# Hybrid block on one core: three weight blocks split early, the mixer's stages in another order

## The chip, the cores and the metric

The kernel runs as one program, launched once, on one core of a Trainium2 chip. The metric is device time in microseconds (us) for the whole program. TensorE (PE) multiplies matrices, VectorE (DVE) and ScalarE (ACT) work on elements, GpSimd (POOL) as well and more slowly, and SyncE (SP) issues most of the DMA transfers. Each engine runs its own instructions strictly in the order in which the program was built; a semaphore wait holds everything behind it on that engine.

## The reference

One residual block on x of 512 frames by 1024 channels, in float32. A gated feed-forward, a mixer and a second gated feed-forward each stand between two RMS norms:

```python
f = swiglu(rmsnorm(x, ffn1_norm_pre[l]), ffn1_w_gu[l], ffn1_w_down[l])
x = x + 0.5 * rmsnorm(f, ffn1_norm_post[l])
m = hybrid_mixer(rmsnorm(x, mix_norm_pre[l]), w_in[l], ...)
x = x + rmsnorm(m, mix_norm_post[l])
f = swiglu(rmsnorm(x, ffn2_norm_pre[l]), ffn2_w_gu[l], ffn2_w_down[l])
x = x + 0.5 * rmsnorm(f, ffn2_norm_post[l])
```

The mixer projects h with `w_in` and splits the columns. Half A is a recurrence with 8 heads of 64 channels, half B a gated, causal, depthwise convolution of width 31 with a layer norm. Both halves go through the output projection `w_out`. The recurrence, for each head and frame:

```python
sz = jnp.einsum('bhij,bhj->bhi', state, z_t)
state = (state * w_t[:, :, None, :]
         + sz[..., None] * b_t[:, :, None, :]
         + v_t[..., None] * k_t[:, :, None, :])
y_t = jnp.einsum('bhij,bhj->bhi', state, r_t)
```

## The kernel before

**Stages.** By time in the profiled execution: the first feed-forward's up products (0 to 241 us), its down product (to about 355, with the norms to 384), the mixer (to about 655), the first column half of the output projection (to 669.6) and the second (to 694), the second feed-forward's up products (to 925) and down product (to 1052).

**Weights.** All large weights lie in DRAM as blocks of 128x1024 float32 (512 KB). `wload` loads one block, `wblock` splits it: ScalarE casts it to a high part (`whi`), VectorE subtracts that from the raw block and gets the low part (`wlo`); with `eng` GpSimd does it instead. `mm3` makes a float32 product of three matmuls, on lines L129, L132 and L133: high by high, low by high, high by low. One block against 512 frames is 24 matmuls of 128x512. `preload` does the same for blocks that a stage needs at its start (`lraw`, `lhi`, `llo`).

**Mixer.** The 8 heads go in four pairs (0 to 3) and two groups of two pairs, G0 and G1; the convolution's 512 channels in four tiles, c0 to c3. A projection block of `w_in` feeds one of key, receptance, value of a pair, or one half of a conv tile's gate. Names in `PLAN`, in the order in which the stages are written:

- `li`, `lg`: the low-rank inputs and the output gate; `p0` to `p3`: projection, token shift (L501 on ScalarE, L502 on VectorE) and score products of a pair. On TensorE the scores are L799 and L807 (out of `bk` and `z`), then L817 (64x64, 128 of them in the trace for a pair) and the value products L778, L779; L783 is the bonus sum, L723 and L725 the decay and rate.
- `c0` to `c3`: a conv tile; `p` puts its 30 shifted multiplications on ScalarE (`cpr`, L681) and the additions on GpSimd (`cacc`, L682), `t` puts the greater part on VectorE (L674).
- `s0`, `s1`: the triangular solve of a group on VectorE (L853 to L870). It reads N, which is sent through DRAM (md, nd, N, D).
- `e0`, `e1`: the solved blocks go through DRAM again (rd, td, Mt, T); TensorE then makes e.P (L903, 32x32 products out of Mt) and, after a copy by ScalarE, e.R (L910, 32x32).
- `k0`, `k1`: combine, L932 (called k.W) and L941 (k.A) on TensorE, masks and sums E on VectorE (L945). `b0`, `b1`: the chain over the 8 chunks (L961, L966) and the heads' norms. `O`, `g0`, `g1`, `x`, `w0`: the conv's norm, mixing, and the start of the output projection.

**What sets the order.** A list scheduler at build time gives each engine one fixed order out of dependencies and a priority per instruction. Priority follows `PLAN`: an item written later comes later, `/n` moves an item by n, `@m` sets it to that of mark m (`m0`, `m1`), and tables such as `O_ST` or `O_CC` move parts of an item. Thus an item that stands later in `PLAN` fills in wherever an earlier one waits.

**Output projection.** The four blocks of the first half are used as 2, 3, 0, 1 (`W_ORDER`); GpSimd makes the low part of blocks 0 and 3 (`POOL_WO`). The second half's four blocks are preloaded raw and split, in the same order. The kernel's norm after it reads the first half's PSUM banks (L252, L256) while the second half begins; PSUM tiles of one tag share two or three buffers (`psum`). Loads on SyncE's queue keep their written order (`load`), also those of x and of the second feed-forward.

Of the kernel before, what the change touches and what calls it, by code (L numbers as in the profile page):

```python
# [8 lines left out]
F32 = mybir.dt.float32  # L9
F32R = mybir.dt.float32r  # L10
# [3 lines left out]
ALU = mybir.AluOpType  # L14
# [4 lines left out]
P = 128  # L19
# [66 lines left out]


def wload(c, i, tag=None):
    if tag is None:
        raw = c.wp.tile([P, 1024], F32, name="wraw", tag="raw", bufs=c.nraw)  # L90
    else:
        raw = slot(c, [P, 1024], F32, "lraw", tag)
    load(c, raw, c.A["w"][i])
    return raw


def wblock(c, i, hi=None, lo=None, raw=None, prev=None, aprev=None, eng=None):

    nc = c.nc
    if raw is None:  # L100
        raw = wload(c, i)
# [349 lines left out]

def ffn_down(c, wbase, gs, gpost, scale, finish, xin, ahead=None):

# [54 lines left out]
DQ = False  # L508
PLAN = 'li p0 p1 c0t320/1000 m1 m0 s0/800 p2 c2p/0 c1p/300 p3 e0@1 s1@0 k0 lg b0 c3t256/600 e1/-150 k1/150 x O g0 b1 w0 g1'
T_SOLVE = ('CB', 'AA')  # L510
T_COMB = ('B', 'A')
COMB_LAG = 3
POOL_PROJ = ()
POOL_WO = (0, 3)
ACT_M = (3, 0, 0, 0)
O_PK = (0, 0, 0, 100)
O_PR = (200, 0, 0, 0)
O_PW = (0, 0, 0, 0)
O_HO = (0, 0, 0, 400)
O_CP = (0, -150)  # L520
O_ST = (-60, 0, -300, 200)
O_CC = (200, -60)
O_SC = (0, 0, 40, -300)
O_PV = (-150, 0, 40, -150)
O_N = (40, 0)
O_T = (-300, 200)
T_PR = 'BBBBC'
# [573 lines left out]
def body(es, tc, A, O, first=True, mixer=True, second=True):  # L1101
# [25 lines left out]
    with phase():  # L1127
# [44 lines left out]

        ffn_down(c, 0, gs, gpo, 0.5, fin, lambda t: load(c, x[t], A["x"][t * P : t * P + P, :]), ahead)
        led = [psum(c, [P, SEQ], tag) for tag in LEAD]
# [145 lines left out]
```

## Time and profile before

| what | value |
|---|---|
| runs (3): median, lowest, highest | 1056.44, 1051.72, 1057.47 us |
| profiled execution, its time | 1054.72 us |
| its span, first to last instruction | 1052.9 us |
| mean granted TensorE clock | 0.981 of full |
| TensorE / VectorE / ScalarE / GpSimd busy | 96% / 74% / 46% / 14% |
| DMA traffic | 107.77 MB, mean 102 GB/s |

Times in the rows are from the span's start. In a timeline a row is one instruction or a run of like ones; the bracket at its end tells how long the engine had been idle before it and what ended that. "PEclk" in windows is the granted clock, 1.00 for full speed; the brackets `(x75)` are counts of instructions.

### The profile page before, as it was taken

How to read it: one execution, taken by the hardware profiler on the slowest of the kernel's cores; microseconds unless marked ns; L12 is line 12 of the kernel's file. 1: busy time of each engine (PE TensorE's matmuls, PEld its weight loads, DVE VectorE, ACT ScalarE, POOL GpSimd, SP SyncE). 2: the span in 40 equal slices, each digit the busy share in tenths (PEclk: the TensorE clock that was granted, in tenths of full speed). 3: DMA queues.
4: the chain of work that ended last, by engine and by line, in shares of the span. 5: the costliest groups of instructions: out<-in, count | busy, mean ns of one | idle time of the engine just before them, and what ended most of it. 6: DMA issues, size and time to landing. Idle time of an engine off the chain costs nothing.

```text
span 1052.9 us, 18597 instructions
## 1 busy us (share of the span) xinstructions
PE 1011.4 (96%) x7570; PEld 892.1 (85%) x7570; DVE 777.1 (74%) x1392; ACT 484.8 (46%) x724; POOL 147.0 (14%) x164
## 2 busy tenths in 40 slices
PE   8999999999999899989988898999999999999997
PEld 8899999998888787757667676788999999988885
DVE  5799989985334756789568797687999899853335
ACT  7453444443224435665766375433534444432232
POOL 0000000000000020365788380000000000000000
PEclk9999999999999999999996989999999999999999
DMA  5233333324425221212420310722333333234231
GB/s 200 81 121 104 117 101 107 100 96 145 150 89 185 86 81 62 77 56 80 91 72 22 61 62 5 271 86 82 120 103 118 101 107 100 96 131 144 89 118 80
DMA packets 54589, 107.77 MB, mean 102 GB/s; under 512 B 28776, under 2 KB 28904, under 8 KB 54504
## 3 DMA queue, kind: packets, MB, share of 16 engines
q1 hardware_dynamic: 53640, 103.96, 30.9%
q10 hardware_dynamic: 864, 2.63, 0.7%
q8 instruction: 59, 0.97, 0.4%
q14 instruction: 26, 0.21, 0.1%
HBM read 98.69 MB, written 7.88 MB: 101 GB/s over the span
## 4 chain that ended last, share of the span: by engine, by line
PE 81%; DVE 10%; ACT 3%; DMA 3%; issue 1%; POOL 1%; SPq 0%; DVEq 0%; ACTq 0%; POOLq 0%
PE ps L129 25%; PE ps L133 25%; PE ps L132 25%; DVE ps L674 1%; DVE wlo L108 1%; PE ps L941 1%; PE ps L817 1%; DMA lraw<-w 1%; POOL cacc L682 1%; DMA D<-nd 1%; DVE E L945 1%; ACT cacc L1033 1%; PE ps L194 1%; DVE llo L108 0%; ACT whi L105 0%
## 5 line engine op out<-in xcount | busy, mean ns | idle before, releaser
L108 DVE TENSOR_TENSOR wlo<-wraw,whi 128x1024 fp32r<-128x1024 f32 x103 | 129.2, 1254 | 138.2 <-ACT whi L105 137.8
L129 PE MATMUL ps<-hT,whi 128*128 128x256 f32 (+1 forms) x600 | 196.2, 329 | 1.1 <-ACT hT L179 0.7
L105 ACT CAST whi<-wraw 128x1024 fp32r<-128x1024 f32 x105 | 110.2, 1050 | 184.9 <-PE ps L132 107.5
L133 PE MATMUL ps<-hT,whi 128*128 128x256 f32 (+1 forms) x600 | 194.4, 326 | 0.4 <-DVE hT L186 0.2
L132 PE MATMUL ps<-hT,wlo 128*128 128x256 f32 (+1 forms) x600 | 194.2, 325 | 0.3 <-DVE ms_s L164 0.3
L682 POOL TENSOR_TENSOR cacc<-cacc,cpr 128x512 f32<-128x512 f32 (+2 forms) x120 | 128.6, 1071 | 33.3 <-ACT cpr L681 25.0
L129 PEld LDWEIGHTS ps<-hT,whi 128*128 128x128 f32 x600 | 114.9, 192 | 14.8 <-issue 3.1
L133 PEld LDWEIGHTS ps<-hT,whi 128*128 128x128 f32 x600 | 114.4, 191 | 11.8 <-issue 1.7
L132 PEld LDWEIGHTS ps<-hT,wlo 128*128 128x128 f32 x600 | 115.0, 192 | 10.4 <-issue 1.5
L132 PE MATMUL ps<-whi,gh 128*128 128x512 f32 x288 | 112.0, 389 | 0.0
L133 PE MATMUL ps<-wlo,gh 128*128 128x512 f32 x288 | 112.0, 389 | 0.0
L681 ACT ACTIVATE cpr<-gpad,vecs 128x512 f32<-128x512 f32 (+2 forms) x120 | 71.1, 601 | 37.4 <-POOL cacc L682 37.0
L132 PE MATMUL ps<-tsum,slo 128*128 128x256 f32 x288 | 80.0, 283 | 0.0
L133 PE MATMUL ps<-tsum,shi 128*128 128x256 f32 x288 | 80.0, 283 | 0.0
L129 PE MATMUL ps<-tsum,shi 128*128 128x256 f32 x288 | 76.3, 283 | 0.0
L129 PE MATMUL ps<-whi,gh 128*128 128x512 f32 x288 | 71.5, 389 | 0.0
L133 PEld LDWEIGHTS ps<-wlo,gh 128*128 128x128 f32 x288 | 54.1, 188 | 11.2
L132 PEld LDWEIGHTS ps<-whi,gh 128*128 128x128 f32 x288 | 54.1, 188 | 11.2
L129 PEld LDWEIGHTS ps<-whi,gh 128*128 128x128 f32 x288 | 53.9, 188 | 11.1
L132 PEld LDWEIGHTS ps<-tsum,slo 128*128 128x128 f32 x288 | 55.3, 192 | 0.0
L133 PEld LDWEIGHTS ps<-tsum,shi 128*128 128x128 f32 x288 | 55.3, 192 | 0.0
L365 ACT CAST shi<-s 128x1024 fp32r<-128x1024 f32 x36 | 37.8, 1050 | 36.0 <-DVE s L358 22.1
(273 smaller groups left out, 2328.0 us busy)
## 6 DMA issues: line engine op xcount, KB each, us to landing
wraw<-w SPq DMA_DIRECT2D x105, 512.0 KB, 3.6
lraw<-w SPq DMA_DIRECT2D x57, 512.0 KB, 3.7
x<-x SPq DMA_DIRECT2D x8, 512.0 KB, 4.5
xs<-x SPq DMA_DIRECT2D x8, 512.0 KB, 2.6
x<-xs SPq DMA_DIRECT2D x8, 512.0 KB, 6.3
gain<-gains ACTq DMA_DIRECT2D x5, 512.0 KB, 5.2
out<-x SPq DMA_DIRECT2D x3, 512.0 KB, 2.6
N<-md SPq DMA_DIRECT2D x4, 256.0 KB, 3.6
```

The lines of the kernel that those rows point to most:

```text
L105: c.last_hi = nc.scalar.copy(hi, raw)
L108: c.last_lo = (eng or nc.vector).tensor_tensor(lo, raw, hi, ALU.subtract)
L129: i = nc.tensor.matmul(out, lhsT=lh, rhs=rh, start=start, stop=False)
L132: nc.tensor.matmul(out, lhsT=ll, rhs=rh, start=False, stop=False)
L133: return nc.tensor.matmul(out, lhsT=lh, rhs=rl, start=False, stop=stop)
L194: i = c.nc.tensor.transpose(out=pt[:, k], in_=self.xn[t][:, kk * P : (kk + 1) * P], identity=c.ident)
L365: nc.scalar.copy(sh, sums)
L674: self.dve_queue(nc.vector.scalar_tensor_tensor(dst, gp[:, j : j + n], dw[:, j : j + 1], lo, ALU.mult, ALU.add), False)
L681: nc.scalar.mul(pr, gp[:, n + j : j + SEQ], dw[:, j : j + 1])
L682: self.pool_queue(nc.gpsimd.tensor_tensor(hi, hi, pr, ALU.add), j == 1)
L817: nc.tensor.matmul(ps[s][dst[par], cc, r], lhsT=bk[g, c0 + cc, s], rhs=E[g, l, par, c0 + cc, 1] if r else I2[g], start=True, stop=True)
L941: nc.tensor.matmul(pa[par][:, cc].rearrange("p a b -> p (a b)"), lhsT=Z_[g, d0 + cc].rearrange("p a b -> p (a b)"), rhs=L_[g, d0 + cc].rea ...
```

## The change

Three blocks of the second half of the output projection (column half two, blocks 0, 1 and 2) are loaded, split and stored to DRAM in the first feed-forward's down product, on GpSimd's DMA queue; block 3 is still loaded raw. The second half then loads high and low parts. `PLAN` puts `p3` ahead of `c1`, `lg` ahead of `k0`, and other offsets follow. `ACT_M` takes four copies of pair 0's masks from ScalarE (the multiplications on VectorE then cover whole tiles), `POOL_PROJ` gives one low part in the projection to GpSimd, `POOL_WO` takes one of two in the output projection away from it.

```diff
+PRE = (26, 27, 28)
+PRE_AT = (1, 3, 5, 7, 9, 11, 13, 15, 17)
+
+def preread(c, todo):
+    if todo:
+        raw = slot(c, [P, 1024], F32, "praw", "sr")
+        c.nc.gpsimd.dma_start(raw, c.A["w"][todo[0]])
+        c.ready.append((todo.pop(0), raw))
+
+def presplit(c, todo):
+    nc = c.nc
+    i, raw = c.ready.pop(0)
+    hi, lo = slot(c, [P, 1024], F32R, "phi", "tmp"), slot(c, [P, 1024], F32R, "plo", "tmp")
+    after(c, nc.scalar.copy(hi, raw), c.last_hi)
+    after(c, nc.vector.tensor_tensor(lo, raw, hi, ALU.subtract), c.last_lo)
+    d = [c.dp.tile([P, 1024], F32, name=f"sp{i}_{n}") for n in range(2)]
+    nc.gpsimd.dma_start(d[0], hi.bitcast(F32))
+    nc.gpsimd.dma_start(d[1], lo.bitcast(F32))
+    c.split[i] = d
+    preread(c, todo)
+
 def wload(c, i, tag=None):
+    if i in c.split:
+        return None
...
 def wblock(c, i, hi=None, lo=None, raw=None, prev=None, aprev=None, eng=None):
+    if i in c.split:
+        if hi is None:
+            c.turns = c.turns % 3 + 1
+            hi, lo = (c.wp.tile([P, 1024], F32R, name="w" + n, tag="raw" if c.turns == 3 else n, bufs=2) for n in ("hi", "lo"))
+        load(c, hi.bitcast(F32), c.split[i][0])
+        load(c, lo.bitcast(F32), c.split[i][1])
+        return hi, lo
...
+    if todo:
+        preread(c, todo), preread(c, todo)
     for k in range(NF - NS):
         w = wblock(c, wd + k)
+        if c.ready and k in PRE_AT:
+            presplit(c, todo)
...
-PLAN = 'li p0 p1 c0t320/1000 m1 m0 s0/800 p2 c2p/0 c1p/300 p3 e0@1 s1@0 k0 lg b0 c3t256/600 e1/-150 k1/150 x O g0 b1 w0 g1'
+PLAN = 'li p0 p1 c0t320/0 s0/800 m1 m0 p2 c2p/600 p3 c1p/600 e0@1 lg k0@1 s1@0 b0 c3t256/0 e1/-400 x k1@1 g0/400 O b1 w0/800 g1'
...
-COMB_LAG = 3
-POOL_PROJ = ()
-POOL_WO = (0, 3)
-ACT_M = (3, 0, 0, 0)
+COMB_LAG = 4
+POOL_PROJ = (11,)
+POOL_WO = (0,)
+ACT_M = (1, 0, 0, 0)
...
-O_ST = (-60, 0, -300, 200)
-O_CC = (200, -60)
+O_ST = (-150, -300, 40, 200)
+O_CC = (400, 0)
...
-        ffn_down(c, 0, gs, gpo, 0.5, fin, lambda t: load(c, x[t], A["x"][t * P : t * P + P, :]), ahead)
+        ffn_down(c, 0, gs, gpo, 0.5, fin, lambda t: load(c, x[t], A["x"][t * P : t * P + P, :]), ahead, [NB_FFN + n for n in PRE])
```

The other tables (`O_PR`, `O_HO`, `O_CP`, `O_PV`, `O_N`, `O_T`) change in the same way.

**TensorE, pair 2's last score products, 489 to 492 us in the trace.** L817 are these products, L129, L132 and L133 the wide ones of a projection block. Before:

```order
L817 MATMUL ps<-I_3958,bk 64x64
L133 MATMUL ps<-hT,whi 128x512
L817 MATMUL ps<-I_3958,bk 64x64 x2
L129 MATMUL ps<-hT,whi 128x512
L817 MATMUL ps<-I_3958,bk 64x64
L132 MATMUL ps<-hT,wlo 128x512
L817 MATMUL ps<-E,bk 64x64
L133 MATMUL ps<-hT,whi 128x512
L817 MATMUL ps<-E,bk 64x64 x3
L129 MATMUL ps<-hT,whi 128x512
L132 MATMUL ps<-hT,wlo 128x512
L133 MATMUL ps<-hT,whi 128x512
```

After (L855 is before's L817, and L163, L166 and L167 are before's L129, L132 and L133):

```order
L855 MATMUL ps<-E,bk 64x64 x2
L855 MATMUL ps<-I_3988,bk 64x64 x2
L855 MATMUL ps<-E,bk 64x64 x2
L855 MATMUL ps<-I_3988,bk 64x64 x2
L855 MATMUL ps<-E,bk 64x64 x2
L163 MATMUL ps<-hT,whi 128x512
L166 MATMUL ps<-hT,wlo 128x512
L167 MATMUL ps<-hT,whi 128x512
L163 MATMUL ps<-hT,whi 128x512
L166 MATMUL ps<-hT,wlo 128x512
L167 MATMUL ps<-hT,whi 128x512
L163 MATMUL ps<-hT,whi 128x512
```

Before, the two kinds alternate. After, the score products stand in a few pieces and the wide ones in others; four changes back and forth are left. (The trace counts each of these small products twice.) The wide ones belong to c1 before and to pair 3's key and receptance after.

**TensorE, from e.P0 to pair 3's scores, 513 to 530 us in the trace.** L903 is e.P0, L799 and L807 the scores of pair 3, L753 the sum for its key's norm. Before:

```order
L723 MATMUL ps<-wa,wup 128x512
L725 MATMUL ps<-wa,wup 128x512
L903 MATMUL ps<-Mt 32x32 x32
L129 MATMUL ps<-hT,whi 128x512
L132 MATMUL ps<-hT,wlo 128x512
L133 MATMUL ps<-hT,whi 128x512
...
L133 MATMUL ps<-hT,whi 128x512
L753 MATMUL ps<-tk,blkones 2x512
L799 MATMUL ps<-bk,z 64x128 x16
L807 MATMUL ps<-I_3958,z 64x64 x16
L129 MATMUL ps<-hT,whi 128x512
```

After (L941 is before's L903, L837 before's L799):

```order
L163 MATMUL ps<-hT,whi 128x512
L166 MATMUL ps<-hT,wlo 128x512
L941 MATMUL ps<-Mt 32x32
L167 MATMUL ps<-hT,whi 128x512
L941 MATMUL ps<-Mt 32x32 x2
L837 MATMUL ps<-bk,z 64x128
L941 MATMUL ps<-Mt 32x32
L837 MATMUL ps<-bk,z 64x128
L941 MATMUL ps<-Mt 32x32
L837 MATMUL ps<-bk,z 64x128
L941 MATMUL ps<-Mt 32x32
L837 MATMUL ps<-bk,z 64x128
```

Before, e.P0 was one piece, and the receptance's block of pair 3 stood between it and the scores. After, e.P0 stands behind two more blocks (value of pair 3, and the first of c1) and alternates with L837 and then L845 (before's L807), product by product: 54 changes in all.

**SyncE's queue, from the last blocks of the first half to the second feed-forward's.** Before:

```order
L74 DMA wraw<-w 128x1024 x2
L74 DMA lraw<-w 128x1024 x6
L74 DMA x<-xs 128x1024 x4
L74 DMA lraw<-w 128x1024 x2
L74 DMA wraw<-w 128x1024 x2
```

After (`sp_0` holds a high part, `sp_1` a low part):

```order
L74 DMA wraw<-w 128x1024 x2
L74 DMA lhi<-sp_0_3057 128x1024
L74 DMA llo<-sp_1_3058 128x1024
L74 DMA lraw<-w 128x1024
L74 DMA lhi<-sp_0_2906 128x1024
L74 DMA llo<-sp_1_2907 128x1024
L74 DMA lhi<-sp_0_2982 128x1024
L74 DMA llo<-sp_1_2983 128x1024
L74 DMA lraw<-w 128x1024 x2
L74 DMA x<-xs 128x1024 x4
L74 DMA lraw<-w 128x1024 x2
L74 DMA wraw<-w 128x1024 x2
```

Before, four raw blocks and the first two of the second feed-forward followed each other. After, six split parts and one raw block stand there, and the second feed-forward's two and x behind them.

## Rows read from the trace of the kernel before

**Rows 1.** Page part 1: busy time, share of the span and count of instructions.

```profile
PE 1011.4 (96%) x7570; PEld 892.1 (85%) x7570; DVE 777.1 (74%) x1392; ACT 484.8 (46%) x724; POOL 147.0 (14%) x164
```

**Rows 2.** Windows: busy us (instructions) per engine, granted clock, DMA share, GB/s.

```profile
235.00:340.00 105.00, 105.00 (x490) 88.06 (x490) 45.20 (x52) 36.41 (x47) 0.00 (x0) 1.00 0.41 136
488.32:508.23 19.91, 19.91 (x191) 11.72 (x190) 13.06 (x40) 10.67 (x16) 15.84 (x12) 1.00 0.23 47
510.00:520.00 10.00, 8.87 (x92) 6.45 (x91) 6.31 (x8) 7.82 (x12) 9.23 (x9) 0.87 0.89 195
...
550.00:560.00 10.00, 6.61 (x144) 6.12 (x144) 5.52 (x8) 9.36 (x16) 8.20 (x7) 1.00 0.22 54
560.00:570.00 10.00, 8.63 (x40) 7.18 (x38) 9.28 (x32) 5.78 (x9) 9.45 (x8) 0.58 0.11 42
...
580.00:590.00 10.00, 6.84 (x47) 5.43 (x44) 9.01 (x36) 1.28 (x2) 3.68 (x3) 0.83 0.00 0
```

**Rows 3.** Chain of waits, 480 to 675: start, us, what.

```profile
488.39 0.95 PE ps L817 x50
...
667.92 1.06 ACT lhi L105
```

**Rows 4.** Timeline of TensorE, 492 to 553: start, us, instruction, idle before.

```profile
492.37 0.39 PE L132 MATMUL ps<-hT,wlo 128*128 128x512 f32 x1
492.60 0.39 PE L133 MATMUL ps<-hT,whi 128*128 128x512 f32 x1
492.92 0.32 PE L817 MATMUL ps<-I,bk 64*64 64x64 f32 x2
493.17 0.50 PE L129 MATMUL ps<-hT,whi 128*128 128x512 f32 x1
493.60 0.33 PE L817 MATMUL ps<-I,bk 64*64 64x64 f32 x2
...
506.79 1.13 PE L783 MATMUL ps<-tk,blkones 128*128 128x512 f32 x2
...
516.41 1.31 PE L903 MATMUL ps<-Mt 32*32 32x32 f32 x62 [1.00 <-DMA Mt<-rd]
...
518.24 0.63 PE L132 MATMUL ps<-hT,wlo 128*128 128x512 f32 x1
518.67 0.63 PE L133 MATMUL ps<-hT,whi 128*128 128x512 f32 x1
...
527.83 1.96 PE L799 MATMUL ps<-bk,z 64*64 64x128 f32 x32 [2.05 <-DVE bk L747]
...
546.84 1.20 PE L910 MATMUL ps<-P,T1p 32*32 32x32 f32 x64 [0.67 <-DVE E L830]
...
552.27 0.41 PE L932 MATMUL ps<-ZT,Mt 64*64 64x64 f32 x4 [2.65 <-POOL cacc L682]
```

**Rows 5.** Timeline of VectorE, 507 to 556: columns as before.

```profile
507.70 1.23 DVE L108 TENSOR_TENSOR wlo<-wraw,whi 128x1024 fp32r<-128x1024 f32 x1 [5.39 <-ACT whi L105]
...
510.16 1.39 DVE L830 TENSOR_TENSOR E<-ps,mask 64x512 f32<-64x512 f32 x2
...
554.93 1.22 DVE L853 TENSOR_TENSOR N<-N,D 128x1024 f32<-128x1024 f32 x1
```

**Rows 6.** Timeline of the DMA queue on SyncE, 509 to 549.

```profile
509.33 0.51 SPq L873 DMA_DIRECT2D td<-T  x1
...
548.07 1.09 SPq L845 DMA_DIRECT2D N<-md  x2
```

**Rows 7.** Timeline of TensorE around the output projection's two halves.

```profile
660.20 0.50 PE L133 MATMUL ps<-wlo,hT 128*128 128x512 f32 x1 [0.22 <-POOL wlo L108]
...
670.88 0.50 PE L129 MATMUL ps<-lhi,hT 128*128 128x512 f32 x1 [1.28 <-DVE ms_s L256]
```

**Rows 8.** Timeline of VectorE there.

```profile
669.00 1.23 DVE L108 TENSOR_TENSOR llo<-lraw,lhi 128x1024 fp32r<-128x1024 f32 x1 [0.74 <-ACT lhi L105]
```

**Rows 9.** Timeline of SyncE's DMA queue there.

```profile
662.39 8.19 SPq L74 DMA_DIRECT2D lraw<-w  x4
```

More of the change, by code (lines that the diff above doesn't have):

```diff
@@ L449, with ffn_down @@
 F2_LATE = 1
-def ffn_down(c, wbase, gs, gpost, scale, finish, xin, ahead=None):
+def ffn_down(c, wbase, gs, gpost, scale, finish, xin, ahead=None, todo=()):
     nc = c.nc
@@ L508 @@
 DQ = False
-PLAN = 'li p0 p1 c0t320/1000 m1 m0 s0/800 p2 c2p/0 c1p/300 p3 e0@1 s1@0 k0 lg b0 c3t256/600 e1/-150 k1/150 x O g0 b1 w0 g1'
+PLAN = 'li p0 p1 c0t320/0 s0/800 m1 m0 p2 c2p/600 p3 c1p/600 e0@1 lg k0@1 s1@0 b0 c3t256/0 e1/-400 x k1@1 g0/400 O b1 w0/800 g1'
 T_SOLVE = ('CB', 'AA')
 T_COMB = ('B', 'A')
-COMB_LAG = 3
-POOL_PROJ = ()
-POOL_WO = (0, 3)
-ACT_M = (3, 0, 0, 0)
+COMB_LAG = 4
+POOL_PROJ = (11,)
+POOL_WO = (0,)
+ACT_M = (1, 0, 0, 0)
 O_PK = (0, 0, 0, 100)
-O_PR = (200, 0, 0, 0)
+O_PR = (0, 100, 0, 0)
 O_PW = (0, 0, 0, 0)
-O_HO = (0, 0, 0, 400)
-O_CP = (0, -150)
-O_ST = (-60, 0, -300, 200)
-O_CC = (200, -60)
+O_HO = (0, -300, 0, 100)
+O_CP = (-60, 0)
+O_ST = (-150, -300, 40, 200)
+O_CC = (400, 0)
 O_SC = (0, 0, 40, -300)
-O_PV = (-150, 0, 40, -150)
-O_N = (40, 0)
-O_T = (-300, 200)
+O_PV = (40, 0, 40, 0)
+O_N = (-60, 40)
+O_T = (0, 400)
 T_PR = 'BBBBC'
@@ L1107, in body @@
     c.nbk, c.ng = 1, 2
+    c.split, c.turns, c.ready = {}, 0, []
     cp = es.enter_context(tc.tile_pool(name="const", bufs=1))
```

## The prediction, on record before the changed kernel ran

> **What bounds the kernel now.** I read the page first. TensorE is busy for 96% of the span, VectorE for 74%, ScalarE for 46% [rows 1]. So time can come from three places: TensorE that is idle, TensorE that is busy but held up, or VectorE where it is late for TensorE. I then asked for windows stage by stage. In the first feed-forward's down product TensorE is busy 105.00 of 105.00 us at full clock, VectorE 45.20, ScalarE 36.41, the DMA engines 0.41 [rows 2]: that stage is TensorE's alone. The mixer (384 to 655 us) is not: in 550 to 560 TensorE is busy 6.61 of 10 and VectorE 5.52, in 560 to 570 VectorE is at 9.28 and the granted clock at 0.58, in 580 to 590 TensorE is at 6.84 and VectorE at 9.01 [rows 2]. There the second triangular solve runs on VectorE, and it cannot begin before N has come through DMA: N is read at 554.93 [rows 5], after its two loads were issued at 548.07 [rows 6], right behind the e.R0 products of 546.84 [rows 4]. So the place of e.R0 sets when VectorE's last long serial piece begins. The timeline of TensorE shows what stands ahead of e.R0, and the timelines around 657 to 671 show two short waits in the output projection [rows 7].
>
> **The change part by part.** All sums are made against the profiled execution, 1054.72 us (span 1052.9), which lies 1.7 us under the median of the runs, 1056.44.
>
> *Splitting three blocks early.* This adds three loads and six stores of 512 KB on GpSimd's queue, three casts of 1.06 us [rows 3] and three subtractions of 1.23 [rows 8], or 3.2 us of ScalarE and 3.7 of VectorE, in a stage where these have 69 and 60 us free of 105 and the DMA engines move 136 GB/s at a share of 0.41 [rows 2]. TensorE's next weight block hides them, so I cost them at 0. If the cover failed, one late block could hold TensorE for the 2.3 us of its cast and subtraction: the bounds are 0 and +2, and nothing there can be gained, since TensorE has no idle in it.
>
> *The second half of the output projection.* Three of its four blocks now arrive split, so three casts and three subtractions go from the stretch before it. TensorE waited 1.28 us at 670.88 for VectorE's reading of a PSUM bank [rows 7]; VectorE was late because it split the last raw block until 670.23 [rows 8], whose load had come last of the four issued from 662.39 [rows 9]. With no split in front, that wait goes. What is late next is the bank's last product itself, some 2 us earlier, so nothing takes the wait's place. The third block's low part in the first half goes from GpSimd back to VectorE: TensorE had waited 0.22 us for it at 660.20 [rows 7]. Gain 1.28 + 0.22 = 1.5. The price is seven loads in place of four on SyncE's queue, the last two behind a gain's load. In the program's order they come ahead of the second feed-forward's blocks and of x. If the last pair were late, all four row groups would wait for it. Before, raw blocks issued at 662.39 and after were split and ready by 670.23 [rows 8, 9], and the new ones need no split; so I take 0, with a bound of +3.
>
> *The order of TensorE's work, part one.* Before, the score products of pair 2 (L817, 64x64) alternate with single 128x512 products of the conv's blocks. Two neighbours of the latter start 0.23 apart (492.37, 492.60), but one with a pair of L817 takes from 492.92 to 493.60, 0.68 us [rows 4]. L817 alone took 0.95 for 50 [rows 3], 0.02 each; so a round trip costs 0.68 - 0.23 - 0.04 = 0.41 more. The stretch 488.32 to 508.23 holds 191 matmuls in 19.91 us, none of it idle [rows 2]. By my count these are 29 wide ones (6.7 us), 128 of L817 (2.4), 2 of L783 (1.1) and 32 small ones (0.6 to 1.0 at L817's rate or half of it), together 11; the other 9 are some 22 round trips. The new order leaves four, 1.6 us. So the stretch ends 7.5 us earlier, near 500.7.
>
> *Part two.* The wide products in that stretch are now pair 3's key and receptance, no longer the conv's two. The key was complete one block (24 x 0.23 = 5.5 us) after the stretch, at 513.9; now it is complete with it, 13 us earlier. VectorE takes it up only after the first solve. That solve is some 2 us later: four copies of pair 0's masks leave ScalarE, and four multiplications of half a tile become whole ones, 4 x 0.7 = 2.8 more by the two that took 1.39 at 510.16 [rows 5], less the 1.2 of one subtraction that goes to GpSimd. So pair 3's scores, for which TensorE waited 2.05 us until 527.83 [rows 4], can run near 517.
>
> *Part three.* TensorE then has two blocks (48 x 0.23 = 11.0) and about 1.8 of small products ahead of e.P0, and comes to it near 513.5. e.P0 needs Mt, which came at 516.4 before, after a wait of 1.00 [rows 4]. The transpose ahead of it was issued at 509.33 [rows 6], behind a weight load that waited for VectorE's subtraction of 507.70 [rows 5]; the new SyncE order has the same pair. I take 517.5, so TensorE waits some 4 us at e.P0 and everything after it on TensorE waits too.
>
> *Part four.* Behind it comes the new interleave: e.P0 (32x32) one by one with pair 3's scores (64x64), 54 changes of shape. The three groups by themselves take 1.3 + 2.0 [rows 4] and about 1.1, 4.4 us. No row shows a change between 32x32 and 64x64. The bounds are 0 and, by the nearest row, half a round trip each: 54 x 0.2 = 11. I take that row, 11. Then 2.4 for the last scores, 2.1 for small products and 9 x 0.23 = 2.1 precede e.R0, at 517.5 + 15.4 + 6.6 = 539.5, 7.3 us before 546.84. With no cost for the changes it would be 528.5.
>
> The Trainium skill, page "TensorEngine Tiling (Array Packing)", section "Key Properties", says that changing the tiling mode drains TensorE. The rows of L817 agree with 0.41 a round trip; for 32x32 against 64x64 no row here shows it. By that rule the sum below stands; without it, the third rival does.
>
> *What it is worth at the end.* N then comes about 7.3 us earlier. VectorE, idle 3.7 of 10 us in 510 to 520 and 4.5 in 550 to 560 [rows 2], can take it up, less the 1.6 of its added work: 5.7. The combine k.W0 that waited 2.65 until 552.27 behind the conv's additions [rows 4] stands ahead of them in the new order and moves as well. The order behind the second solve is nearly unchanged, so I carry 5.7 to the end; bounds -13 (changes free, capped by VectorE's idle time) and +8 (second rival). Other moved offsets I cost at 0, bounds of 1 each way.
>
> **Sum:** -1.5 - 5.7 = -7.2: 1047.5 for the profiled execution, 1049 on the scale of the median.
>
> **The rivals.**
> *VectorE or the combine gives it back.* From 560 on VectorE is over 9 of 10 busy [rows 2], and the first combine's additions share it with the second solve. If these run no earlier, only the junction's 1.5 remains: 1055. For it: VectorE's load from 560. Against: its 4.5 idle us just before.
> *The wait at e.P0 slows TensorE.* After the 1.00 us wait of 516.41, wide products started 0.43 apart instead of 0.23 (518.24, 518.67) [rows 4], and the granted clock of 510 to 520 is 0.87 [rows 2], part of it at the lower of the two levels, 1.2 GHz. If the new 4 us wait brings that on and the 22 us up to e.R0 run at half speed, e.R0 comes near 561, 14 late; at two thirds of that, since small products suffer less, the kernel is 9.5 late less 1.5, 1064. It decides from e.R0 later than 549. Against: the same window, with that wait in it, still shows 0.87 as a whole.
> *The 32/64 changes are free.* e.R0 at 528.5, capped at 13: -14.5, 1042.
>
> **How the numbers follow.** Forecast 0.48, own range 1046 to 1051; given back 0.22; slow clock 0.16; free changes 0.14. I call no change what lies within 0.5%, 1051.2 to 1061.7, about what a measurement of this kernel can tell. Faster: 0.46 of the forecast's and the third rival's 0.14, 0.60; same: 0.22 and 0.02 of the forecast, 0.24; slower 0.16. The range 1041 to 1062 leaves out half of the slow case and more, about 0.12, and 0.05 at the low end.
>
> **What would show it.** In the new trace: no idle on TensorE near the start of the second half; L817's pair-2 group in one piece of about 1 us; e.P0 waiting for Mt near 517; the e.P0 and score interleave 15 us long; e.R0 near 539; N read near 547; the output projection starting some 6 us earlier. Steps are wrong if the interleave takes 5 us, if Mt comes after 522, or if N is earlier and the second solve's end is not. A granted clock under 0.8 between 515 and 540 speaks for the slow rival; a weight load that is late in the second half for the junction's bound.

## The result, and the profile after

The changed kernel takes 1064.75 us (median of five runs, 1062.84 to 1066.41) against 1056.29 for the kernel before on the same chip (five runs). The ratio is 1.0083, with a 95% interval of 1.0057 to 1.0109: it is 8.5 us slower, where 7 us faster was forecast, and outside the range. The profiled execution of after took 1066.41 us (span 1064.4), that of before 1054.72: 11.7 apart, and the readings below are of these two executions; they place 11.1 of the 11.7. The change moved lines down by 34 to 38: L903 of before (e.P) is L941, L910 (e.R) is L948, L799 and L807 (pair 3's scores) are L837 and L845, L682 (the conv's additions on GpSimd) is L720, L862 and L865 (the solve's steps) are L900 and L903, L853 (N) is L891.

Part 1 of after's page answers to [rows 1]: there are as many TensorE instructions as before, and they are busy for 10 us more.

```profile
PE 1021.6 (96%) x7570; PEld 900.5 (85%) x7570; DVE 787.8 (74%) x1392; ACT 483.2 (45%) x720; POOL 148.0 (14%) x173
```

This table sets the same events of both timelines side by side.

| event (us from the span's start) | before | after | difference |
|---|---|---|---|
| e.R0 on TensorE | 546.84 | 546.61 | -0.2 |
| N read on VectorE (the second solve begins) | 554.93 | 552.74 | -2.2 |
| the solve's last step, T on VectorE | 588.62 | 596.00 | +7.4 |
| e.R1 on TensorE | 605.9 | 614.95 | +9.1 |
| end of the mixer's last chain | 639.9 | 651.4 | +11.5 |
| first transposes behind the output projection | 687.4 | 697.18 | +9.8 |
| third group of them | 706.1 | 717.2 | +11.1 |

So the output projection repaid 1.7 and the stage behind it took 1.3 of that again by its third group; all else arose between N and the end of the chain; the last 0.6 of the 11.7 came later still. First the part ahead of N. This is TensorE's timeline of after, with start, us, instruction, repetitions, and idle time ahead with what ended it.

```profile
499.68 0.69 PE L761 MATMUL ps<-wa,wup 64*128 64x512 f32 x1
...
518.16 0.25 PE L941 MATMUL ps<-Mt 32*32 32x32 f32 x4 [1.70 <-DMA Mt<-rd]
518.34 0.43 PE L837 MATMUL ps<-bk,z 64*64 64x128 f32 x2
518.70 0.24 PE L941 MATMUL ps<-Mt 32*32 32x32 f32 x2
518.87 0.43 PE L837 MATMUL ps<-bk,z 64*64 64x128 f32 x2
519.23 0.24 PE L941 MATMUL ps<-Mt 32*32 32x32 f32 x2
...
520.02 0.31 PE L941 MATMUL ps<-Mt 32*32 32x32 f32 x2
520.26 0.68 PE L837 MATMUL ps<-bk,z 64*64 64x128 f32 x2
520.88 0.31 PE L941 MATMUL ps<-Mt 32*32 32x32 f32 x2
...
546.61 1.20 PE L948 MATMUL ps<-P,T1p 32*32 32x32 f32 x64
...
613.91 1.12 PE L1052 MATMUL ps<-ident,cacc 128*128 128x128 f32 x4 [1.08 <-POOL cacc L720]
...
680.53 0.39 PE L167 MATMUL ps<-wlo,hT 128*128 128x512 f32 x1
680.75 0.47 PE L163 MATMUL ps<-lhi,hT 128*128 128x512 f32 x1
```

Read here that the stretch of pair 2's scores ends at 499.7, where 508.2 stood [rows 2]; that e.P0, after a first pair of its products at 515.79, waits for Mt until 518.16; and that one round trip between e.P0 and pair 3's scores takes 0.53 us (518.16, 518.70, 519.23) and then 0.85 (520.02, 520.88). The windows of after show a lower clock in the second case. Columns: stretch, its length, busy us (instructions) of TensorE, weight loads, VectorE, ScalarE and GpSimd, granted clock, DMA share, GB/s.

```profile
510.00:520.00 10.00, 6.70 (x33) 3.56 (x31) 9.29 (x9) 7.21 (x12) 7.73 (x6) 0.97 0.75 125
520.00:530.00 10.00, 10.00 (x52) 5.57 (x52) 5.39 (x6) 4.06 (x7) 3.79 (x3) 0.50 0.31 101
530.00:540.00 10.00, 10.00 (x126) 7.58 (x125) 1.02 (x4) 3.50 (x7) 2.82 (x4) 0.50 0.19 28
...
610.00:620.00 10.00, 8.92 (x116) 6.59 (x112) 8.65 (x13) 8.23 (x16) 6.76 (x8) 0.50 0.16 55
```

From 520 to 540 TensorE was granted the lower of its two levels, 1.2 GHz, throughout; it fell at 519.4, 1.2 us into the interleave and behind two waits for Mt (1.60 ahead of 515.79, 1.70 ahead of 518.16), and was at 1.00 again from 540. The interleave ends near 538.0, 19.8 us after it began, and TensorE's gain of 8.5 from the first stretch is gone by e.R0.

Now the part from N to T. N came 2.2 earlier though e.R0 came only 0.2 earlier: before, VectorE had stood at `lg`'s token shift, waiting 6.98 for ScalarE until 554.26, and took up N behind it (the first line of before, below); in after N follows e.R0 by 6.1 us, before by 8.1. The solve takes 33.7 us before (554.93 to 588.62) and 43.3 after. This is VectorE's timeline of after. L66 to L68 are Newton steps of a reciprocal square root on 128x8 values for the heads' norm of group 0 (the end of b0), placed between the solve's steps; wherever nothing held them they took 0.15 to 0.17.

```profile
552.74 1.22 DVE L891 TENSOR_TENSOR N<-N,D 128x1024 f32<-128x1024 f32 x1 [7.41 <-DMA N<-md]
...
554.46 0.67 DVE L701 SCALAR_TENSOR_TENSOR gpad<-cpr,ps 128x512 f32<-128x512 f32 x1
...
584.82 1.26 DVE L66 TENSOR_TENSOR rs_w<-rs_y 128x8 f32<-128x8 f32 x1
586.00 0.24 DVE L900 TENSOR_TENSOR stmp<-N,ps 128x96 f32<-128x96 f32 x1
586.16 1.28 DVE L67 SCALAR_TENSOR_TENSOR rs_w<-rs_w,gs 128x8 f32<-128x8 f32 x1
587.36 0.25 DVE L903 TENSOR_TENSOR ps<-ps,stmp 128x96 f32<-128x96 f32 x1
...
596.00 0.68 DVE L908 TENSOR_TENSOR T<-ps,D 128x512 f32<-128x512 f32 x1
```

Two lines of VectorE's timeline of before belong to it:

```profile
554.26 0.75 DVE L502 SCALAR_TENSOR_TENSOR wa<-ps,vecs,wa 128x511 f32<-128x511 f32 x1 [6.98 <-ACT wa L501]
...
588.62 0.68 DVE L870 TENSOR_TENSOR T<-ps,D 128x512 f32<-128x512 f32 x1
```

And this is GpSimd's timeline of after, followed by the one of before (its last row is for a later section).

```profile
556.68 12.17 POOL L720 TENSOR_TENSOR cacc<-cacc,cpr 128x512 f32<-128x512 f32 x9 [11.82 <-ACT cpr L719]
569.17 22.36 POOL L720 TENSOR_TENSOR cacc<-cacc,cpr 128x512 f32<-128x512 f32 x16 [0.32 <-ACT cpr L719]
```

```profile
555.93 27.91 POOL L682 TENSOR_TENSOR cacc<-cacc,cpr 128x512 f32<-128x512 f32 x20 [0.99 <-ACT cpr L681]
597.20 2.38 POOL L108 TENSOR_TENSOR wlo<-wraw,whi 128x1024 fp32r<-128x1024 f32 x1 [13.37 <-ACT whi L105]
```

Read across these. The conv's block c1 got its gate (gpad) at 554.46, where it had come at 537.90: c1's wide products now run behind e.R0, and the gate stands behind N on VectorE. So GpSimd sat idle for 11.8 us and made 25 of c1's 30 additions from 556.7 to 591.5, right under the Newton steps, where before all 30 had ended at 583.8. Nine 128x8 operations between 579.7 and 591.5, eight Newton steps and the shift (L64) ahead of them, took 0.60 to 1.29 us, together 10.4, where 9 x 0.16 = 1.4 would do. Before, the same nine took 2.4, because the shift alone took 1.14 under the last addition; so they account for 8.0 of the solve's 9.6 us more. The rest isn't taken apart; c1's gate, 0.67, now stands in the solve too. The solve's own steps between them, with an operand in PSUM, stayed at 0.22 to 0.27.

The rest, from 7.4 to 11.5: c1's last additions run until 613.9, and TensorE waits 1.08 for them ahead of e.R1 (613.91 above), with a granted clock of 0.50 in 610 to 620 (the windows' last row); then c3's gate and the last combine follow late.

### The profile page after: what moved, and what is told of

Read it like the earlier page. It is cut to its first block, busy times and chain, and to the rows that moved or that the text cites. A ratio compares the mean times of both kernels' runs of the same rounds, so it can differ in the third digit from the quotient of the medians.

```text
span 1064.4 us, 18618 instructions
## 1 busy us (share of the span) xinstructions
PE 1021.6 (96%) x7570; PEld 900.5 (85%) x7570; DVE 787.8 (74%) x1392; ACT 483.2 (45%) x720; POOL 148.0 (14%) x173
## 4 chain that ended last, share of the span: by engine, by line
PE 79%; DVE 11%; DMA 3%; ACT 2%; POOL 2%; issue 1%; SPq 1%; DVEq 0%; ACTq 0%; POOLq 0%
PE ps L163 24%; PE ps L166 24%; PE ps L167 24%; POOL cacc L720 2%; DVE ps L712 1%; PE ps L837 1%; DVE ps L903 1%; DMA N<-md 1%; DVE stmp L900 1%; DVE wlo L142 1%; PE ps L228 1%; PE ps L970 1%; PE ps L941 1%; DVE E L868 1%; PE ps L845 1%
## 5 line engine op out<-in xcount | busy, mean ns | idle before, releaser
L163 PE MATMUL ps<-hT,whi 128*128 128x256 f32 (+1 forms) x600 | 196.1, 329 | 0.9 <-ACT hT L213 0.5
L166 PE MATMUL ps<-hT,wlo 128*128 128x256 f32 (+1 forms) x600 | 194.4, 325 | 1.4 <-DVE wlo L142 1.4
L167 PE MATMUL ps<-hT,whi 128*128 128x256 f32 (+1 forms) x600 | 194.2, 326 | 0.2 <-DVE hT L220 0.2
L720 POOL TENSOR_TENSOR cacc<-cacc,cpr 128x512 f32<-128x512 f32 (+2 forms) x120 | 125.3, 1044 | 54.4 <-ACT cpr L719 46.6
L163 PEld LDWEIGHTS ps<-hT,whi 128*128 128x128 f32 x600 | 115.5, 193 | 15.0 <-issue 3.3
L166 PEld LDWEIGHTS ps<-hT,wlo 128*128 128x128 f32 x600 | 115.8, 193 | 11.8 <-DVE wlo L142 1.9
L167 PEld LDWEIGHTS ps<-hT,whi 128*128 128x128 f32 x600 | 115.2, 193 | 12.0 <-issue 2.6
L166 PE MATMUL ps<-whi,gh 128*128 128x512 f32 x288 | 112.0, 389 | 0.0
L167 PE MATMUL ps<-wlo,gh 128*128 128x512 f32 x288 | 112.0, 389 | 0.0
L166 PE MATMUL ps<-tsum,slo 128*128 128x256 f32 x288 | 80.0, 283 | 0.0
L167 PE MATMUL ps<-tsum,shi 128*128 128x256 f32 x288 | 80.0, 283 | 0.0
L163 PE MATMUL ps<-tsum,shi 128*128 128x256 f32 x288 | 76.3, 283 | 0.0
L163 PE MATMUL ps<-whi,gh 128*128 128x512 f32 x288 | 71.5, 389 | 0.0
L166 PEld LDWEIGHTS ps<-whi,gh 128*128 128x128 f32 x288 | 54.1, 188 | 11.2
L167 PEld LDWEIGHTS ps<-wlo,gh 128*128 128x128 f32 x288 | 54.1, 188 | 11.2
L163 PEld LDWEIGHTS ps<-whi,gh 128*128 128x128 f32 x288 | 53.9, 188 | 11.1
L166 PEld LDWEIGHTS ps<-tsum,slo 128*128 128x128 f32 x288 | 55.3, 192 | 0.0
L167 PEld LDWEIGHTS ps<-tsum,shi 128*128 128x128 f32 x288 | 55.3, 192 | 0.0
L399 ACT CAST shi<-s 128x1024 fp32r<-128x1024 f32 x36 | 37.8, 1050 | 36.0 <-DVE s L392 22.1
```

The source lines that it names most:

```text
L163: i = nc.tensor.matmul(out, lhsT=lh, rhs=rh, start=start, stop=False)
L166: nc.tensor.matmul(out, lhsT=ll, rhs=rh, start=False, stop=False)
L167: return nc.tensor.matmul(out, lhsT=lh, rhs=rl, start=False, stop=stop)
L399: nc.scalar.copy(sh, sums)
L720: self.pool_queue(nc.gpsimd.tensor_tensor(hi, hi, pr, ALU.add), j == 1)
```

## The experiments

The first theory was that the time is lost in two steps: the interleave of e.P0 with the scores, which takes the half clock and delays c1, and then GpSimd's additions under the Newton steps. Against it stood that the early split, the planner's new order of the tail, or the clock alone does it. Each kernel starts from the changed one unless said otherwise; ratios are to the kernel before.

**e.P0 and the scores in pieces.** One offset puts pair 3's scores behind e.P0 instead of between its products.

```diff
-O_SC = (0, 0, 40, -300)
+O_SC = (0, 0, 40, -200)
```

> The changed kernel with one offset of pair 3's scores (O_SC) set to -200 instead of -300: on TensorE e.P0 then stands in one piece and pair 3's scores in another, with 18 wide products behind them; the rest of the order changes little. Theory A (the interleave, run at the lower clock for 20 us, ate the gain, and the late c1 did the rest): the two pieces take 5 us instead of 20, e.R0 comes near 536 to 538 instead of 546.6, c1's gate 8 us earlier, and the kernel takes 1053 to 1057. Rival 1 (the wait for Mt ahead of e.P0 lowers the clock whatever follows): the granted clock of 520 to 540 stays at 0.5, e.R0 comes after 544 and the kernel takes 1061 to 1065. Rival 2 (only GpSimd's additions for c1 matter, by when they end): the time follows their end, not e.R0.

Measured: 1056.23 us, ratio 1.0010 [0.9999, 1.0021]. This is TensorE's timeline of that kernel, and then its windows.

```profile
517.78 1.91 PE L941 MATMUL ps<-Mt 32*32 32x32 f32 x62 [1.02 <-DMA Mt<-rd]
519.62 3.68 PE L837 MATMUL ps<-bk,z 64*64 64x128 f32 x32
523.09 1.40 PE L845 MATMUL ps<-I,z 64*64 64x64 f32 x32
```

```profile
510.00:520.00 10.00, 7.22 (x85) 4.76 (x86) 9.30 (x9) 7.15 (x12) 7.86 (x6) 0.85 0.73 130
520.00:530.00 10.00, 10.00 (x156) 8.91 (x154) 5.83 (x11) 8.40 (x15) 7.59 (x8) 0.81 0.50 129
530.00:540.00 10.00, 10.00 (x121) 8.05 (x118) 6.48 (x9) 7.66 (x12) 8.07 (x8) 1.00 0.17 55
```

Two finer windows of it:

```profile
519.60:523.00 3.40, 3.40 (x34) 3.38 (x34) 2.24 (x3) 3.34 (x6) 1.35 (x2) 0.50 0.54 155
524.40:530.00 5.60, 5.60 (x96) 4.57 (x94) 2.92 (x8) 4.09 (x8) 5.29 (x5) 1.00 0.64 145
```

The same three groups take 6.6 us (517.78 to 524.41) instead of 19.8, e.R0 stands at 540.4, c1's gate at 533.3, GpSimd's additions end at 579.1 and the solve takes 33.9 us, to 580.1. In the five kernels that alternate (after, and four of those below) the granted clock of 520 to 530 was 0.50 to 0.58 and of 530 to 540 0.50. In the seven with the groups in pieces it was 0.73 to 0.92 and 0.88 to 1.00. The waits at e.P0 are in both kinds, and behind them the lower level comes in both: with the pieces the clock was 0.50 from 517.78 to 523.00 as well, but 1.00 again from 524.40. So the alternation isn't shown to bring the half clock; what it does is keep it, for 20 us in place of 5. And 16 us gained at T are only 8.5 at the end: something behind the solve takes the rest.

**c1's additions left out.** The edit leaves out ScalarE's shifted multiplications for c1 with them.

```diff
-                for j in range(1, 31):
+                for j in range(1, 31 if ct != 1 else 2):
```

> The changed kernel with 29 of the 30 shifted multiplications and additions of conv tile c1 left out, so that ScalarE and GpSimd are free of them. Theory A's second half (GpSimd's late additions for c1 hold VectorE's small operations in SBUF from 580 to 591, and the last five hold e.R1 until 614): the operations of 128x8 that took 1.2 us take 0.17, the second solve ends near 588 instead of 596.0, e.R1 starts near 605 instead of 615, and the kernel takes 1053 to 1057. Rival 1 (only the half clock of 520 to 540 cost time): 1061 to 1065, the second solve's end within 2 us of 596.

Measured: 1062.05 us, 1.0063 [1.0048, 1.0078]. VectorE's timeline:

```profile
583.06 0.16 DVE L66 TENSOR_TENSOR rs_w<-rs_y 128x8 f32<-128x8 f32 x1
583.18 0.25 DVE L900 TENSOR_TENSOR stmp<-N,ps 128x91 f32<-128x91 f32 x1
583.35 0.16 DVE L67 SCALAR_TENSOR_TENSOR rs_w<-rs_w,gs 128x8 f32<-128x8 f32 x1
...
587.78 0.68 DVE L908 TENSOR_TENSOR T<-ps,D 128x512 f32<-128x512 f32 x1
```

With GpSimd idle from 559 to 593 the steps take 0.16, N to T takes 33.5 us (554.27 to 587.78), and T comes 8.2 earlier than in after. This shows what c1's late work costs the solve, 9.8 us; that it is GpSimd's part of it and not ScalarE's rests on the next experiment. The time itself missed the expectation and lies in its rival's range: of the 8.2, 6.0 are left at the first transposes behind the output projection (691.19 against 697.18), 3.6 at the third group of them and 2.7 in the median of the runs. What is lost between these groups comes as it does with the split alone, below: a wait of 2.83 ahead of the second group, and that group at the lower clock.

**The Newton steps' value in PSUM.**

```diff
-    w = c.sm.tile([P, n], F32, name="rs_w", tag=f"rsw{n}", bufs=2)
+    w = c.sm.tile([P, n], F32, name="rs_w", tag=f"rsw{n}", bufs=2) if at is None else at[:, 2, :n]
...
-        y = rsqrt_many(c, s)
+        y = rsqrt_many(c, s, y2)
```

> The changed kernel with one of the two scratch tiles of the heads' reciprocal root (rs_w, 128x8) placed in the PSUM bank of the squares, which is dead by then. Theory A (an operation whose operands all lie in SBUF waits for GpSimd's running addition, one with an operand in PSUM does not): of the seven operations of 1.2 us between 580 and 591 those that read rs_w take 0.2, the second solve ends 3 to 5 us earlier, and the kernel takes 1060 to 1062. Rival (these operations are long for another reason): their lengths and 1065 stay.

Measured: 1062.16 us, 1.0063 [1.0043, 1.0083]. VectorE's timeline:

```profile
579.05 1.25 DVE L66 TENSOR_TENSOR ps<-rs_y 128x8 f32<-128x8 f32 x1
...
580.40 0.16 DVE L67 SCALAR_TENSOR_TENSOR ps<-ps,gs 128x8 f32<-128x8 f32 x1
...
581.28 0.16 DVE L68 SCALAR_TENSOR_TENSOR rs_y<-ps,rs_y 128x8 f32<-128x8 f32 x1
```

What decides is where the inputs lie. L66 reads both from SBUF and can wait, though it now writes to PSUM: the three of them took 1.25, 0.17 and 0.55. L67 and L68 have one input in PSUM, and all six took 0.15 to 0.17. The shift (L64), with its one input in SBUF, took 0.96. N to T takes 37.8 us, 5.5 less than in after. Of the gain at T (7.2, with 1.7 of it from an earlier N), 1.5 is left at the chain's end (649.9), but 5.8 at the first transposes (691.34): the chain's end alone doesn't set the time.

**The early split alone, over the kernel before.** All offsets and the stages' order as before, the split kept.

```diff
-PLAN = 'li p0 p1 c0t320/0 s0/800 m1 m0 p2 c2p/600 p3 c1p/600 e0@1 lg k0@1 s1@0 b0 c3t256/0 e1/-400 x k1@1 g0/400 O b1 w0/800 g1'
+PLAN = 'li p0 p1 c0t320/1000 m1 m0 s0/800 p2 c2p/0 c1p/300 p3 e0@1 s1@0 k0 lg b0 c3t256/600 e1/-150 k1/150 x O g0 b1 w0 g1'
...
-O_PR = (0, 100, 0, 0)
+O_PR = (200, 0, 0, 0)
...
```

> The kernel before with the early split of three blocks alone: PLAN, POOL_WO and all tables as before. The prediction's term: the wait of 1.28 us at the second half of the output projection is gone, the first feed-forward's down product as long as before: 1055. Rival 1 (the split costs the first stage time): 1057 to 1060. Rival 2 (another wait takes its place): 1056.

Measured: 1058.69 us, 1.0036 [1.0021, 1.0050].

**The new order without the split.**

```diff
-PRE = (26, 27, 28)
+PRE = ()
```

> The changed kernel without the early split (PRE empty); PLAN and all tables as changed. Theory A, with what the split alone has shown (3 us longer than before, through a longer wait and a lower clock around the second feed-forward's first transposes): 1061 to 1065, the interleave at a clock of 0.5 again. Rival (the split's gain at the junction, 1.5 us, holds in this order, and is lost here): 1066.

Measured: 1065.74 us, 1.0077 [1.0055, 1.0099]. So the order makes the whole loss by itself. The rival's 1066 is the nearer value, but the ratio lies within after's interval, so what the split is worth in this order stays open. In the old order the split alone costs 0.2 to 0.5%. There the second half starts with no wait (its first product at 670.25), as forecast, but the next wait is longer. TensorE's timeline, of before and then of the split alone, and VectorE's of the split alone:

```profile
695.82 1.09 PE L194 MATMUL ps<-ident,fg 128*128 128x128 f32 x8 [1.94 <-DVE fg L171]
```

```profile
695.99 1.97 PE L228 MATMUL ps<-ident,fg 128*128 128x128 f32 x8 [2.83 <-DVE fg L205]
```

```profile
693.98 0.69 DVE L286 SCALAR_TENSOR_TENSOR fg<-ps,gain 128x512 f32<-128x512 f32 x1 [0.63 <-ACT ms_j L174]
...
694.65 1.28 DVE L205 SCALAR_TENSOR_TENSOR fg<-x,rs_y,gain 128x1024 f32<-128x1024 f32 x1
```

The transposes need fg (L205), and VectorE now makes it behind the last eviction of the projection (L286), where before it stood ahead of that. Behind the longer wait the group takes 1.97 in place of 1.09: the granted clock there (690 to 700) is 0.83, and was 1.00 before. By the third group the kernel is 2.2 later than before, though it came 0.7 earlier to the first. The same happens in five more of the fourteen traces (c1's additions left out, c1's block ahead of pair 3, the gate alone, c3 ahead of b0, the pieces with the PSUM value): in these six VectorE has the two in this order, the wait is 2.82 or 2.83 and the lower clock follows; in the other eight fg stands first and the wait is 1.4 to 1.9.

**c1's block ahead of pair 3.**

```diff
-PLAN = '... p2 c2p/600 p3 c1p/600 e0@1 ...'
+PLAN = '... p2 c2p/600 c1p/600 p3 e0@1 ...'
```

> The changed kernel with c1 ahead of p3 in PLAN again, all else as changed. e.P0 then stands in one piece ahead of pair 3's receptance, and the score products of pair 2 alternate with c1's wide ones as before. Theory A (the interleave of e.P0 with pair 3's scores, which only p3's move makes, cost the 8.5 us): 1055 to 1058, e.R0 near 547, granted clock of 520 to 540 over 0.9. Rival (the other tables cost it): 1062 or more.

Measured: 1068.71 us, 1.0111 [1.0094, 1.0129], the slowest of all, and the expectation missed by over 10 us. The gate came at 539.0, the planner put e.P0 in one piece and N to T took 32.8 us, as the theory has it; but e.R0 came at 549.3 and N only at 557.3, and behind the solve a new alternation arose, of e.P1 with another 64x64 group. TensorE's timeline:

```profile
604.67 0.33 PE L1030 MATMUL ps<-I,Yb 64*64 64x64 f32 x2
604.92 0.24 PE L941 MATMUL ps<-Mt 32*32 32x32 f32 x2
605.10 0.33 PE L1030 MATMUL ps<-I,Yb 64*64 64x64 f32 x2
```

It lasts from 603.9 to 609.4, at a granted clock of 1.00 (0.67 in 610 to 620), and T to the chain's end takes 62.6 us, where before took 51.3. Its 5.5 us can be only a part of that; c3's gate comes at 614.4, and the longer wait for fg follows. How these share the loss isn't shown. A cure for the first loss is not a cure if the planner builds the next one.

**What stands behind the solve.** In all kernels of the new order T to the chain's end took 55 to 64 us. Four kernels ask why. The first keeps the alternation and restores the old tail (the plan from e0 on, the combine's lag and six offsets).

```diff
-PLAN = '... e0@1 lg k0@1 s1@0 b0 c3t256/0 e1/-400 x k1@1 g0/400 O b1 w0/800 g1'
+PLAN = '... e0@1 s1@0 k0 lg b0 c3t256/600 e1/-150 k1/150 x O g0 b1 w0 g1'
-COMB_LAG = 4
+COMB_LAG = 3
-O_CP = (-60, 0)
+O_CP = (0, -150)
...
```

> The changed kernel with PLAN behind e0 and the tables that act there (COMB_LAG, O_HO, O_CP, O_ST, O_CC, O_N, O_T) as before; e.P0 and pair 3's scores still alternate. The time from the second solve's end to the second chain's end was 51.3 us before, 55.4 changed and 60.5 with the pieces alone. Theory B (what the pieces gain is lost again by the new order behind the solve, where c3's gate stands behind e.R1's copies on ScalarE): this segment comes back to 50 to 53, the solve ends at 596 as changed, and the kernel takes 1060 to 1063. Rival (the segment is long because of the clock alone): still 55 or more, 1065.

The second does that with the groups in pieces (the diff above and the one of O_SC).

> The same with O_SC at -200, so that e.P0 and pair 3's scores stand in pieces. If the two causes add up, the second solve ends near 580 and the segment takes 50 to 54: 1046 to 1051, faster than both kernels. Rival (the clock, or GpSimd's additions, take back what the order gives): 1055 or more.

The third has the pieces and, of the old tail, the offset of the conv's gate alone.

```diff
-O_CP = (-60, 0)
+O_CP = (0, -150)
...
-O_SC = (0, 0, 40, -300)
+O_SC = (0, 0, 40, -200)
```

> The pieces with one more constant as before, O_CP = (0, -150): on ScalarE c3's gate then stands ahead of e.R1's copies; ho's products and e.R1 alternate in part as with the pieces. Theory B: c3's gate 3 to 8 us earlier than 605.5 and the segment 55 or less: 1050 to 1054. Rival (the gate's place is not what makes it long): 1055 to 1058.

The fourth has the pieces and puts c3 ahead of b0.

```diff
-PLAN = '... s1@0 b0 c3t256/0 e1/-400 ...'
+PLAN = '... s1@0 c3t256/600 b0 e1/-400 ...'
```

> The pieces, with c3 ahead of b0 in PLAN and its shifted operations later by 600: TensorE makes c3's two blocks between the first combine's products, some 20 us earlier, and its gate no longer stands behind e.R1's copies. Theory (the gain of the pieces, 6 us at the second solve's end, is lost because c3's convolution waits for its gate while VectorE idles from 583 to 606): 1048 to 1052. Rival (the convolution then gets into the second solve's way on VectorE): 1056 or more.

The first two make a table of four with after and the pieces (medians and ratios).

| | new tail | old tail |
|---|---|---|
| alternation | 1064.75, 1.0083 [1.0057, 1.0109] | 1063.36, 1.0063 [1.0042, 1.0084] |
| in pieces | 1056.23, 1.0010 [0.9999, 1.0021] | 1051.99, 0.9957 [0.9943, 0.9971] |

The gate alone gave 1054.90, 0.9989 [0.9976, 1.0003]; c3 ahead of b0 1059.65, 1.0030 [1.0014, 1.0046], with a granted clock of 0.50 to 0.67 in 580 to 630; both missed what their theory expected and came out nearer their rivals. So the alternation costs 0.7 to 1.1% (8 to 11 us), and the new tail another 0.5% with the pieces; the 0.2% with the alternation is within the intervals. None of the four kernels in the table has the longer wait for fg. In pieces with the old tail it is the fastest kernel of this study: 4.5 us faster than before, which beats both, and 1 us above the range expected for it. A candidate for a cause in the tail stands in ScalarE's timeline, first of the kernel in pieces with the new tail, then with the old one.

```profile
604.36 1.16 ACT L950 COPY Mt<-ps 32x512 f32<-32x512 f32 x2 [8.93 <-PE ps L948]
605.54 0.60 ACT L698 ACTIVATE cpr<-ps 128x512 f32<-128x512 f32 x1
```

```profile
601.70 0.60 ACT L698 ACTIVATE cpr<-ps 128x512 f32<-128x512 f32 x1 [4.26 <-PE ps L167]
...
603.63 1.16 ACT L950 COPY Mt<-ps 32x512 f32<-32x512 f32 x2
```

In the new tail c3's gate (L698) stands behind the copies of e.R1, which wait 8.93 us for TensorE; in the old one it goes first, 3.8 us earlier. With the gate alone moved, c3's gpad came at 601.7 in place of 606.2, and T to the chain's end took 58.6 in place of 60.5; the first transposes came 2.6 earlier (684.28 against 686.86), about as early as with the whole old tail (684.92), and by the third group, behind the longer wait for fg, that is gone (705.92 against 705.34). So the gate may be most of the tail's cost, but its time alone doesn't show it. I had expected 50 to 53 with the old tail, and it took 57.2 (in pieces) and 55.2 (alternating): the direction holds, the size doesn't.

**Two that combine.** The pieces together with the PSUM value (the diffs of both, above):

> Both edits: e.P0 and pair 3's scores in pieces, and rs_w of the heads' reciprocal root in PSUM. With the pieces alone the second solve ends at 580.1, but tile c3's gate is ready only at 605.5 and its convolution ends as late as before. If that convolution sets the end, the second edit gives nothing: 1055 to 1057. Rival (the gains add up, since GpSimd's additions hold VectorE there too): 1053 to 1054.

Measured: 1062.53 us, 1.0060 [1.0038, 1.0081], 6 us slower than the pieces alone. The chain ends no later (639.5 against 640.6), so it loses behind it. The last transposes of the conv's norm stand at 645.60, against 640.98 in the pieces alone, behind a wait of 1.73 for ScalarE; the first transposes behind the projection come at 690.3 against 686.9, and the longer wait for fg (2.82, at 699.62) with the lower clock behind it makes up the rest, 6.6 by the third group. Why the planner's order of the conv's norm differs isn't settled. And the fastest kernel without the split (`PRE = ()`, as above):

> The fastest kernel so far (e.P0 and the scores in pieces, the old order behind the solve; 1052.0) without the early split of three blocks. If the split is worth its junction, the wait of 1.3 us at the second half comes back: 1053 to 1055. Rival, as the split alone over the kernel before has shown (3 us longer): 1048 to 1051.

Measured: 1052.64 us, 0.9972 [0.9960, 0.9985]. The wait at the second half comes back, as 0.76. The ratios differ by 0.0015 (1.6 us) in the split's favour, but the intervals overlap, so a gain of the split isn't shown.

## Why the prediction was wrong

**Right, with their sizes.** Pair 2's stretch ended at 499.7 (forecast 500.7). Mt released e.P0 at 518.16 (517.5). The wait at the start of the second half went (680.53 to 680.75 with no gap). The split's cost at nothing in the first feed-forward nearly held: the first transposes behind it stand at 355.8 against 355.7, the last at 378.0 against 377.1. What was said to come next in the second half, "nothing takes the wait's place", was wrong in the kernel with the split alone, where the wait for fg grew from 1.94 to 2.83.

**Mis-sized: part four.** "54 changes" at 0.2 each, with the products, gave 15.4 us; it took 19.8. At the first round trips' 0.53 the 27 of them would come to 14.3, close to the forecast; at the lower clock those with L837 took 0.85 and those with L845 0.64. e.R0 came 7.1 after the forecast's 539.5: 0.7 of it from Mt, 4.4 from the interleave and 2.0 from what stands behind it, which took 8.6 in place of 6.6. The clock was in the list of rivals and not in the sum. The rival had it follow the long wait at e.P0; it did come behind the waits, but with the pieces it lasted 5 us behind much the same waits, and with the alternation 20. e.R0 came at 546.61, so that rival's own condition, "e.R0 later than 549", was not met, although its 1064 is the time measured. That agreement is chance: its loss was to arise ahead of e.R0, and the real one arose behind N.

Two smaller terms of the step to N were wrong as well. "4 x 0.7 = 2.8 more" counts the whole tiles' multiplications in full; the half tiles had taken 0.42 each, so it is 1.1 more, less the 1.2. That the first solve still ended 1.8 later (503.43 against 501.63), as forecast, has some other reason and is luck. And N before was held for 2 us by `lg`'s shift on VectorE, not by e.R0 alone; that gave N most of its 2.2.

The Trainium skill, page "TensorEngine Tiling (Array Packing)", section "Key Properties", says that a change of the tiling mode drains TensorE. For 32x32 against 64x64 the trace now agrees: 19.8 us alternating, 6.6 in pieces, of the same products, though with the lower clock for different lengths of time.

**Failed: what it is worth at the end.** "The order behind the second solve is nearly unchanged, so I carry 5.7 to the end", with other moved offsets at "0, bounds of 1 each way". N did come earlier, by 2.2, and the solve then lost 9.6, of it 8.0 because c1's additions had moved from ahead of the Newton steps to under them. Leaving c1's additions out gave the solve its 33.5 us back, and a PSUM input freed single steps; together they show it. The error in method: I followed the moved work on TensorE and VectorE, and costed GpSimd's only as something TensorE waits for. What GpSimd does to VectorE while both run was in the trace of before: one Newton step took 2.39 us there, as VectorE's timeline of before shows, under the GpSimd subtraction of 597.20, the last row of that fence further up. I had not looked for it.

```profile
597.02 0.17 DVE L68 SCALAR_TENSOR_TENSOR rs_y<-rs_w,rs_y 128x8 f32<-128x8 f32 x1
597.22 2.39 DVE L66 TENSOR_TENSOR rs_w<-rs_y 128x8 f32<-128x8 f32 x1
```

The Trainium skill, page "SBUF — State Buffer", section "SBUF: two separate sides", says that a VectorE operation with two SBUF inputs and a GpSimd operation that reads SBUF exclude each other for the whole instruction. The rows agree in the main: up to 1.29 us with both inputs in SBUF, 0.16 with one in PSUM, against GpSimd additions of 22.36 / 16 = 1.4 each. One L66 with both inputs in SBUF took 0.17 among such additions.

**Also missed: the tail.** The offsets behind the solve that I costed at 0 were worth 0.5% by the table of four, with the groups in pieces.

**Open.** Why T to the chain's end still takes 55 to 57 us with the old tail, where before takes 51.3. Why the clock in 700 to 710 was 0.86 in after, which has the shorter wait for fg, and 1.00 in before and in pieces. How much of the alternation's 8 to 11 us is the changes of shape and how much the clock. An estimate: at the higher level a round trip took 0.53 with L837 (first trips of after) and 0.43 with a 64x64 group (604.67 to 605.10 with c1's block ahead of pair 3), so the 16 and 9 trips of after would take about 12.4; then some 7 of the 19.8 are the clock.

## What to carry to other kernels

When work is moved in a planned order, follow every engine's share of it to the time at which it now runs, and ask which operations of the other engines it then lies beside; here a chain of GpSimd additions that ran on 8 us longer cost VectorE 8. Group small matmuls by shape: alternating two tile shapes, with the lower clock that stayed on, tripled the time of the same products. Where a planner sets the order, check the row order after each fix, since one moved block makes it build another alternation elsewhere.

## What the runs showed of the hardware

- Alternating 32x32 and 64x64 products: 0.53 us a round trip at a granted clock of 1.00, 0.85 at 0.50 (L837 in after).
- During the alternation TensorE is busy 10.00 of 10.00 us by the profile, and its clock still stays at 0.50, for 20 us in after (0.50 to 0.58 and 0.50 in the two windows of each of five kernels). With the same products in pieces it was 0.50 for 5 us behind the waits, then 1.00. One alternation of 5.5 us (c1's block ahead of pair 3) ran at 1.00.
- In six traces TensorE waited 2.82 or 2.83 us for fg, and the eight transposes behind it took 1.87 to 1.97 us in place of 1.09 to 1.10.
- A 128x8 VectorE operation with both inputs in SBUF took mostly 1.2 to 1.3 us beside GpSimd's additions (0.55 and 0.60 once each, and once 0.17), and 0.16 without; one input in PSUM was enough to free it. The 128x8 shift, with one input in SBUF, took 0.96 to 1.14 beside them and 0.16 without.
